# A decoder trunk on one core: the down projection also computed with seven block products for eight

## The chip, the cores and the metric

The kernel runs on one core of a Trainium2 chip. The metric is the device time of one execution in microseconds. TensorE does the matmuls, VectorE (DVE in the rows) and ScalarE (ACT) the element-wise work, GpSimd (POOL) little, and SyncE (SP) issues all loads of weights from HBM. An engine executes its instructions in program order; engines wait for each other by semaphores.

## The reference, cut to what matters

Two layers act on 256 tokens of width 2048. Layer 0 is a state-space mixer, layer 1 an attention over shared keys and values; each is followed by the same feed-forward part, and a norm ends the whole:

```
def swiglu(u, w_gate, w_up, w_down):
    return (jax.nn.silu(u @ w_gate) * (u @ w_up)) @ w_down
...
        u = rmsnorm(h, g_ffn[i])
        h = h + swiglu(u, w_gate[i], w_up[i], w_down[i])
```

D_FF is 5632, so gate and up are 2048 x 5632 matrices and down is 5632 x 2048, all float32. The change concerns the product with `w_down`, in both layers.

## The kernel before, in words

**Jobs.** The matmul work is a list of jobs (`add`), run in order by `run_stream` (lines 146 to 155). A job usually owns one weight tile of 512 input rows by 512 output columns, 1 MB, laid out as 128 partitions x 4 blocks (`kb`) x 512. For float32 accuracy each operand is split in two parts, hi (rounded to fp32r, by a ScalarE copy) and lo (the rest, by a VectorE subtraction), and a product is three matmuls: hi x hi, lo x hi, hi x lo (`mm3`, lines 128 to 137). The activations are the stationary operand (128 x 128), the weights the moving one (512 columns). A tile has 4 blocks and two halves of 128 tokens (`a`), so a job is 4 x 2 x 3 = 24 matmuls.

**Split and load.** `split_upto` (lines 96 to 115) splits a tile in two units of 128 x 1024: hi on ScalarE (line 111), lo on VectorE (line 112). The hi and lo buffers hold four units, so a unit's buffer is free when the matmuls of the unit four before are done. Tiles come through a ring of three `raw` buffers, loaded by SP (line 90), asked for two jobs ahead of their split. The order on every engine is the order of the program: matmuls of job i, then `split_ahead(i)` (lines 118 to 126; the split of job i+1, and of a further job where both together have at most three units), then the callbacks hung on job i (`pend`, `after`).

**Gate and up.** The 5632 hidden columns are 11 chunks of 512, done in two halves of 6 and 5 chunks (`PARTS`); after the chunks of a half come the down jobs that read them. The first chunk is 8 plain jobs. The other ten of each layer have 13 jobs: in the first weight tile of gate and up, seven block products stand in for eight (a 2 x 2 block scheme over token halves, halves of the tile's 4 blocks, and gate/up). These seven products (`s_add`, `mm1`, 6 matmuls each, one unit) are at the indices 0, 1, 2, 4, 6, 7, 8 of the chunk as products 1, 6, 7, 5, 2, 3, 4; they read sums of weights made by VectorE in tiles E, F, W (`s_sum`, line 769; T4 is made just ahead of the split of product 4) and sums of activations made once per layer (`s_combine`). The plain jobs are at 3, 5 and 9 to 12. `s_evac` combines results (line 803). `g_rows` (lines 844 to 853) transposes a chunk's result into the operand `g` of the down jobs: four transposes on TensorE, a ScalarE copy to hi (line 852) and a VectorE sub to lo (line 853), for token half 0 behind the job at index 2 of the next chunk, for half 1 behind that at index 3.

**Down.** Before, `ffn` (lines 877 to 921) has a plain loop: four column tiles c, and for each the 6 or 5 tiles of the half, each job with 24 matmuls into two banks of PSUM. Behind a column `add_hr` (two VectorE ops, line 875) adds the result to h. In layer 0's second half, `u_chunk` then transposes the new columns of h for the k jobs of the attention (`hT_blocks`, lines 169 to 181: TensorE, ScalarE line 179, VectorE line 180). PSUM has eight banks: acc0 to acc3, two x, two tr; consecutive chunks alternate between the acc banks (`own`) and x and tr.

The pool `rows` (9 buffers of 128 x 512) holds results between steps; a buffer is handed out again after as many allocations as the pool has.

Of the kernel before, what the change touches and what calls it, by code (L numbers as in the profile page):

```python
# [30 lines left out]
def trunk_kernel(ctx: ExitStack, tc: tile.TileContext, par, x_tok, x_grp, b_st, g_st, c_st, cst, gvec,  # L31
# [5 lines left out]
    keep = ctx.enter_context(tc.tile_pool(name="keep", bufs=1))  # L37
    big = ctx.enter_context(tc.tile_pool(name="big", bufs=1))
    ring = ctx.enter_context(tc.tile_pool(name="ring", bufs=2))
    rows = ctx.enter_context(tc.tile_pool(name="rows", bufs=9))  # L40
    ps = ctx.enter_context(tc.tile_pool(name="ps", bufs=1, space=bass.MemoryType.PSUM))
    ctx.enter_context(tc.manual_schedule())

# [29 lines left out]
    def add(src, t, mm, after=None):  # L73
        j = Job()
        j.src, j.t, j.mm, j.after, j.pre = src, t, mm, after or [], []
        j.part, j.make = None, None
        jobs.append(j)
        return j

# [5 lines left out]
    def load_upto(n):  # L85
        while st["load"] < min(n, len(jobs)):
            j = jobs[st["load"]]
            if j.part is None:
# [7 lines left out]
    def split_upto(n):  # L96
        while st["split"] < min(n, len(jobs)):
            i = st["split"]
            load_upto(i + 3)
            if len(parts) < 2:  # L100
                parts.append([ring.tile([128, 4, 512], F32R, name=f"{nm}{i}", tag=nm) for nm in ("hi", "lo")])
            j = jobs[i]
            if j.make is not None:
                j.make()
            j.hi, j.lo = [], []
            for p in range(units(j)):
                raw = j.raw[:, 2 * p:2 * p + 2] if j.part is None else j.part()
                u = st["unit"]
                st["unit"] += 1
                hi, lo = [t[:, 2 * (u % 2):2 * (u % 2) + 2] for t in parts[u // 2 % 2]]  # L110
                act.activation(hi, raw, AF.Copy)  # L111
                (pool if i < NPRE else dve).tensor_tensor(lo, raw, hi, op=OP.subtract)  # L112
                for k in range(2):
                    j.hi.append(hi[:, k])
                    j.lo.append(lo[:, k])
            st["split"] += 1
# [22 lines left out]
    def mm1(pr, opnd, j, first, join):  # L139
        for kb in range(2):  # L140
# [3 lines left out]
            pe.matmul(pr, oh, j.lo[kb], start=False, stop=first and kb == 1, skip_group_check=join)  # L144

    def run_stream(i0, i1):
        for i in range(i0, i1):
# [36 lines left out]

    def s_combine(un, g):

        SC["c"] = big.tile([128, 2, 4, 2, 128], F32R, name=f"sc_{un}", tag="DA"[un == "u_f1"])
# [500 lines left out]
    def chunk_end(j, f):  # L688
        pend.append((j, f))
# [39 lines left out]

    CT, NT, T, gr = {}, [], {}, {}  # L730

    def gu_acc(nm, own):
# [123 lines left out]
    def r_diag(r):  # L856
        t = row()
# [19 lines left out]
    def ffn(l, un, wg, wu, wd, r, down_evac):  # L877
        for hf, (ca, cb) in enumerate(PARTS):
            for c in range(ca, cb):
                own = (cb - 1 - c) % 2  # L880
                j0 = len(jobs)
                if c == 0:
                    for nm, w in (("gate", wg), ("up", wu)):
                        for kg in range(4):
                            add(w, 4 * c + kg, gu_job(nm, un, own, kg, kg == 0, kg == 3))
                    pend.append((j0 + 4, gate_evac(c, r)))
                    pend.append((j0 + 7, gu_end))
                    pend.append((j0 + 8, up_evac(c)))
                    src = lambda a, c=c: (lambda: sil[c][a])
                else:  # L890
                    pend.append((j0 - 5, s_load(l, c, wg, wu)))
                    pend.append((j0 - 3, S_T1))
                    pend.append((j0 - 2, S_T2))
                    pend.append((j0 - 2, S_T3))
                    X = lambda nm, w, kg: add(w, 4 * c + kg, gu_job(nm, un, own, kg, kg == 1, kg == 3, (0,) if nm == "gate" else (0, 1)))
                    for i in (1, 6, 7):
                        s_add(i, un, own)
                    X("gate", wg, 1)
                    s_add(5, un, own)
                    X("gate", wg, 2)  # L900
# [12 lines left out]
            for c in range(4):  # L913
                for kg in range(k0, k1):
                    add(wd, 11 * c + kg, mm_job(("down", l, hf, c), kg == k0, kg == k1 - 1, g_opnd(l, hf), 4 * (kg - k0)))
                if hf == 0:
                    chunk_end(len(jobs), lambda c=c: add_hr(("down", l, 0, c), c, r))
                else:
                    chunk_end(len(jobs), down_evac(c))
                    if l == 0:  # L920
                        u_chunk(len(jobs) + 1, c, "u_kv", 0)

    def down0_evac(c):
        def f():
# [427 lines left out]
```

## Time and profile before

| what | value |
|---|---|
| median of 3 runs | 2098.48 us (2096.45 to 2098.67) |
| profiled execution, own time | 2097.13 us |
| its span, first to last instruction | 2095.3 us |
| mean granted TensorE clock | 0.995 |
| busy: TensorE, VectorE, ScalarE | 2061.8, 1387.9, 1000.5 us |

The difference between the profiled execution's time and its span is 1.83 us; the median of the runs lies 1.35 us above the profiled one. In the rows further down a timeline row has the start in microseconds from the span's start, the duration, the engine, the line of the kernel, the operation, out<-in, the shape, and in brackets how long the engine had been idle before and what released it. Matmuls are pipelined: one lasts longer than the distance to the next.

### The profile page before, as it was taken

Reading aid. Unit: us, or ns where it says so; the run is one execution under the profiler, and the core shown is the slowest. Engines: PE = TensorE matmul, PEld = TensorE weight load, DVE = VectorE, ACT = ScalarE, POOL = GpSimd, SP = SyncE. Lnnn points to the kernel's source line nnn. Section 1 sums busy time; section 2 is a strip of 40 time slices with the busy share of each in tenths; the row PEclk is TensorE's granted clock in tenths of the full one; section 3 lists DMA queues with packets and bytes.
Section 4 is the critical chain, followed back from the end, with each engine's and each line's share of the span. In section 5 each row is a group of like instructions: output and inputs, shape, how many; then the busy total and the mean of one; then the engine's idle time right before and its main releaser. Section 6 shows DMA issues by size and latency. Waiting matters only on the chain.

```text
span 2095.3 us, 28782 instructions
## 1 busy us (share of the span) xinstructions
PE 2061.8 (98%) x11592; PEld 1736.3 (83%) x11592; DVE 1387.9 (66%) x1941; ACT 1000.5 (48%) x1253; POOL 149.9 (7%) x105
## 2 busy tenths in 40 slices
PE   7999999999999999999999999999999999999998
PEld 6778778888888888889999998788888888888886
DVE  8984977776456777555555555667777546777654
ACT  6344555544434455444444444555455334555443
POOL 7741400000000000000000000000000000000000
PEclk9999999999999999999999999999999999999999
DMA  3034556554565555555544544464564556554454
GB/s 142 23 122 144 199 200 221 188 194 161 201 227 196 179 182 180 201 183 177 183 161 168 178 163 165 172 221 168 199 227 150 199 186 224 215 189 173 174 200 149
DMA packets 54054, 376.20 MB, mean 180 GB/s; under 512 B 6432, under 2 KB 6944, under 8 KB 9120
## 3 DMA queue, kind: packets, MB, share of 16 engines
q1 hardware_dynamic: 53920, 374.36, 50.9%
q8 instruction: 91, 1.49, 0.3%
q14 instruction: 43, 0.35, 0.0%
HBM read 370.14 MB, written 2.10 MB: 178 GB/s over the span
## 4 chain that ended last, share of the span: by engine, by line
PE 92%; DVE 5%; ACT 1%; issue 1%; DMA 1%; SPq 1%; ACTq 0%; POOLq 0%; POOL 0%; DVEq 0%
PE acc L137 16%; PE acc L135 16%; PE acc L136 16%; PE x L137 3%; PE x L135 3%; PE x L136 3%; PE tr L135 3%; PE tr L137 3%; PE tr L136 3%; PE acc L961 3%; PE acc L960 3%; PE acc L959 3%; PE x L524 1%; PE acc L144 1%; PE acc L142 1%; PE acc L143 1%
## 5 line engine op out<-in xcount | busy, mean ns | idle before, releaser
L112 DVE TENSOR_TENSOR lo<-raw,hi 128x1024 fp32r<-128x1024 f32 x594 | 721.1, 1241 | 341.9 <-ACT hi L111 337.2
L111 ACT ACTIVATE hi<-raw 128x1024 fp32r<-128x1024 f32 x608 | 627.2, 1055 | 346.9 <-PE acc L136 248.6
L135 PE MATMUL acc<-hi,g 128*128 128x512 f32 x704 | 274.9, 390 | 0.0
L137 PE MATMUL acc<-lo,g 128*128 128x512 f32 x704 | 274.0, 389 | 0.0
L136 PE MATMUL acc<-hi,g 128*128 128x512 f32 x704 | 274.0, 389 | 0.0
L135 PE MATMUL acc<-hi,u_f 128*128 128x512 f32 x512 | 200.5, 392 | 0.6 <-ACT hi L111 0.5
L137 PE MATMUL acc<-lo,u_f 128*128 128x512 f32 x512 | 199.6, 390 | 0.5 <-DVE lo L112 0.5
L136 PE MATMUL acc<-hi,u_f 128*128 128x512 f32 x512 | 199.4, 389 | 0.0
L137 PEld LDWEIGHTS acc<-lo,g 128*128 128x128 f32 x704 | 132.2, 188 | 27.6
L136 PEld LDWEIGHTS acc<-hi,g 128*128 128x128 f32 x704 | 132.2, 188 | 27.1
L135 PEld LDWEIGHTS acc<-hi,g 128*128 128x128 f32 x704 | 132.2, 188 | 27.0
L111 ACT ACTIVATE hi<-st 128x1024 fp32r<-128x1024 f32 x60 | 63.4, 1056 | 115.2 <-DVE st L769 115.2
L137 PEld LDWEIGHTS acc<-lo,u_f 128*128 128x128 f32 x512 | 96.1, 188 | 21.3 <-DVE lo L112 1.3
L135 PEld LDWEIGHTS acc<-hi,u_f 128*128 128x128 f32 x512 | 96.1, 188 | 20.8 <-ACT hi L111 0.9
L135 PE MATMUL x<-hi,u_f 128*128 128x512 f32 x288 | 113.0, 392 | 0.0
L136 PEld LDWEIGHTS acc<-hi,u_f 128*128 128x128 f32 x512 | 96.2, 188 | 20.0 <-DVE u_f L180 0.3
L137 PE MATMUL x<-lo,u_f 128*128 128x512 f32 x288 | 112.2, 390 | 0.0
L136 PE MATMUL x<-hi,u_f 128*128 128x512 f32 x288 | 112.1, 389 | 0.0
L135 PE MATMUL tr<-hi,u_f 128*128 128x512 f32 x288 | 112.0, 389 | 0.0
L136 PE MATMUL tr<-hi,u_f 128*128 128x512 f32 x288 | 112.0, 389 | 0.0
L137 PE MATMUL tr<-lo,u_f 128*128 128x512 f32 x288 | 112.0, 389 | 0.0
L112 DVE TENSOR_TENSOR lo<-st,hi 128x1024 fp32r<-128x1024 f32 x60 | 73.4, 1223 | 25.7 <-ACT hi L111 24.1
(294 smaller groups left out, 3792.7 us busy)
## 6 DMA issues: line engine op xcount, KB each, us to landing
raw<-w_down SPq DMA_DIRECT2D x88, 1024.0 KB, 4.8
raw<-w_gate SPq DMA_DIRECT2D x68, 1024.0 KB, 4.9
raw<-w_up SPq DMA_DIRECT2D x68, 1024.0 KB, 4.9
raw<-w_kv SPq DMA_DIRECT2D x32, 1024.0 KB, 4.8
su<-w_up SPq DMA_DIRECT2D x20, 1024.0 KB, 4.8
sg<-w_gate SPq DMA_DIRECT2D x20, 1024.0 KB, 7.0
raw<-w_glu SPq DMA_DIRECT2D x16, 1024.0 KB, 4.8
raw<-w_q SPq DMA_DIRECT2D x16, 1024.0 KB, 4.8
```

The source lines that it names most:

```text
L111: act.activation(hi, raw, AF.Copy)
L112: (pool if i < NPRE else dve).tensor_tensor(lo, raw, hi, op=OP.subtract)
L135: pe.matmul(pr, oh, j.hi[kb], start=first and kb == 0 and not jn, stop=False, skip_group_check=jn)
L136: pe.matmul(pr, ol, j.hi[kb], start=False, stop=False, skip_group_check=jn)
L137: pe.matmul(pr, oh, j.lo[kb], start=False, stop=last and kb == 3 and not jn, skip_group_check=jn)
L142: pe.matmul(pr, oh, j.hi[kb], start=first and kb == 0, stop=False, skip_group_check=join)
L143: pe.matmul(pr, ol, j.hi[kb], start=False, stop=False, skip_group_check=join)
L144: pe.matmul(pr, oh, j.lo[kb], start=False, stop=first and kb == 1, skip_group_check=join)
L524: pe.matmul(yb[64 * g2:64 * g2 + 64, g], H[q][r, ri, gl + g2].rearrange("p k c -> p (k c)"), Z[r, :, ri, 2 * (8 * o + g) + b], start=ri == ...
L959: pe.matmul(p, j.hi[kb][:, s], u[:, 0], start=first and kb == 0 and n % 2 == 0, stop=False)
L960: pe.matmul(p, j.hi[kb][:, s], u[:, 1], start=False, stop=False)
L961: pe.matmul(p, j.lo[kb][:, s], u[:, 0], start=False, stop=last and kb == 3 and n % 2 == 1)
```

## The change

Tiles of down are taken in pairs of column tiles (c = 2cp and 2cp + 1). For each pair, the four weight tiles of the half's first two row tiles form a 2 x 2 block matrix, and seven products replace its eight (token halves x row tiles x column tiles). It does so for seven of the eight pairs; the last pair of layer 1 stays plain.

- `down_pair` makes the jobs. A product (`s_job`) has 12 matmuls (`mm1` with n = 4); an `x_job` is a plain tile. The order is written out: `1 B2 5 A2 3 B3 7 6 A3 2 4 B4 A4 A5 B5` (digits are products, A and B the columns), or up to `A4 B4` in the second half. Three of the four weight tiles are loaded whole into E, F and W (`d_load`, three jobs ahead), the fourth through the ring. `whole` makes weight sums on VectorE (two ops of 128 x 1024 each), just ahead of the splits of products 5, 7, 6 and 4. `e1`, `e6`, `e7` and `fold` combine the results (one ScalarE copy, seven VectorE ops a pair).
- `g_combine` makes the sums of activations, called from `g_rows` in the first two chunks of each half: n = 0 and 1 for the first chunk's token halves, 2 and 3 for the second's. It needs the transposed bank `tr`.
- The pool `rows` has 6 buffers, not 9; there are new tiles Q, X0, X1. The parity of `own` in the second halves turns over, and the pairs alternate between the acc banks and x and tr.
- Both `add_hr` of a pair come at its end (behind its last job and the job after), and both `u_chunk` one and two jobs later.

```
-    rows = ctx.enter_context(tc.tile_pool(name="rows", bufs=9))
+    rows = ctx.enter_context(tc.tile_pool(name="rows", bufs=6))
...
+            if c - PARTS[hf][0] < 2:
+                g_combine(2 * (c - PARTS[hf][0]) + a, tr, dst[:, :, b0:b0 + 4])
...
+    def g_combine(n, tr, g):
...
+        def put(i, src):
+            d = SC["g"][i // 2]
+            act.activation(d[:, 0, i % 2], src, AF.Copy)
+            dve.tensor_tensor(d[:, 1, i % 2], src, d[:, 0, i % 2], op=OP.subtract)
+
+        if n == 0:
+            act.activation(X0, tr, AF.Copy)
+        if n == 1:
+            act.activation(X1, tr, AF.Copy)
+            dve.tensor_tensor(X0, tr, X0, op=OP.subtract)
+            put(2, X0)
+        if n == 3:
+            V = v4(row())
+            dve.tensor_tensor(X1, X1, tr, op=OP.subtract)
+            put(0, X1)
+            dve.tensor_tensor(V, tr, X0, op=OP.subtract)
+            put(1, V)
+            t0 = slice(0, 128)
+            dve.tensor_tensor(X0, g[:, 0, :, t0].bitcast(F32), V, op=OP.subtract)
+            dve.tensor_tensor(X0, X0, g[:, 1, :, t0].bitcast(F32), op=OP.add)
+            put(3, X0)
...
+    def d_load(l, hf, cp, wd):
+        def f():
+            k0 = PARTS[hf][0]
+            for t, c, k in (("E", 0, 0), ("F", 1, 0), ("W", 1, 1)):
+                T[t] = big.tile([128, 4, 512], F32, name=f"d{t}{l}{hf}{cp}", tag=t)
+                nc.sync.dma_start(T[t], wd[11 * (2 * cp + c) + k0 + k].rearrange("p (k n) -> p k n", k=4))
+        return f
...
+    def down_pair(l, hf, cp, wd, own, r):
...
+        pend.append((j0 - 3, d_load(l, hf, cp, wd)))
...
+            j = add(wd, 11 * 2 * cp + ca + 1, f)
+            if i != 2:
+                j.home = {1: E, 5: E, 3: W, 7: F, 6: W, 4: W}[i]
+            j.make = {5: whole(E, E, F), 7: whole(F, F, W), 6: whole(W, E, W)}.get(i)
...
+        order = "1 B2 5 A2 3 B3 7 6 A3 2 4 B4 A4 A5 B5" if hf == 0 else "1 B2 5 A2 3 B3 7 6 A3 2 4 A4 B4"
...
+        def e1():
+            T["P"] = row()
+            act.activation(T["P"], acc[keys[0]][0], AF.Copy)
+
+        def e6():
+            T["u"] = row()
+            tt(T["u"], T[6], T["P"], OP.subtract)
+            tt(T["P"], T[5], T["u"], OP.add)
+
+        def e7():
+            t = row()
+            tt(t, T[7], T["P"], OP.add)
+            dve.scalar_tensor_tensor(T["u"], T[7], -1.0, T["u"], op0=OP.mult, op1=OP.subtract)
+            T["x"] = t
+
+        pend.append((pos["1"], e1))
+        pend.append((pos["6"], e6))
+        pend.append((pos["A3"], e7))
+        pend.append((pos["4"], lambda: (fold(T["P"], 0, 1), fold(T["u"], 1, 0))))
+        pend.append((pos["4"] + 1, lambda: fold(T["x"], 1, 1)))
...
-                own = (cb - 1 - c) % 2
+                own = (c + 1) % 2
...
+                down_pair(l, hf, cp, wd, (cp + hf + 1) % 2, r)
+                n = len(jobs)
+                for i in range(2):
+                    c = 2 * cp + i
+                    if hf == 0:
+                        chunk_end(n - 1 + i, lambda c=c: add_hr(("down", l, 0, c), c, r))
+                    else:
+                        chunk_end(n - 1 + i, down_evac(c))
+                        if l == 0:
+                            u_chunk(n + 1 + i, c, "u_kv", 0)
```

## Rows read from the trace of the kernel before

**Rows 1.** The page's busy times and shares by engine, over the span.
```profile
span 2095.3 us, 28782 instructions
...
PE 2061.8 (98%) x11592; PEld 1736.3 (83%) x11592; DVE 1387.9 (66%) x1941; ACT 1000.5 (48%) x1253; POOL 149.9 (7%) x105
```

**Rows 2.** One stretch: us; PE, PEld, DVE, ACT, POOL busy (x); clock; DMA.
```profile
600.00:800.00 200.00, 200.00 (x895) 165.62 (x894) 143.95 (x139) 96.62 (x102) 0.00 (x0) 1.00 0.58 206
```

**Rows 3.** TensorE's waits, 200 to 1500 us: total, times, longest.
```profile
PE acc L135 <- ACT hi L111: 5.8, 3, 3.7
```

**Rows 4.** Timeline of TensorE, first and last matmul of the first down tile.
```profile
514.05 0.39 PE L135 MATMUL acc<-hi,g 128*128 128x512 f32 x1
...
519.26 0.39 PE L137 MATMUL acc<-lo,g 128*128 128x512 f32 x1
```

**Rows 5.** Timeline of ScalarE and VectorE in the first down tiles.
```profile
516.23 2.35 DVE L112 TENSOR_TENSOR lo<-raw,hi 128x1024 fp32r<-128x1024 f32 x2
...
531.29 1.06 ACT L111 ACTIVATE hi<-raw 128x1024 fp32r<-128x1024 f32 x1 [1.66 <-PE acc L136]
...
532.38 1.23 DVE L112 TENSOR_TENSOR lo<-raw,hi 128x1024 fp32r<-128x1024 f32 x1 [1.27 <-ACT hi L111]
```

**Rows 6.** Timeline of one gate/up chunk, three engines, index 3 to 6.
```profile
391.88 0.68 DVE L853 TENSOR_TENSOR g<-acc,g 128x512 fp32r<-128x512 f32 x1
...
395.99 0.69 DVE L853 TENSOR_TENSOR g<-acc,g 128x512 fp32r<-128x512 f32 x1 [0.56 <-ACT g L852]
...
396.56 0.39 PE L135 MATMUL x<-hi,u_f 128*128 128x512 f32 x1
...
396.94 1.23 DVE L112 TENSOR_TENSOR lo<-sg,hi 128x1024 fp32r<-128x1024 f32 x1 [0.26 <-ACT hi L111]
398.08 0.68 DVE L803 TENSOR_TENSOR row<-tr,row 128x512 f32<-128x512 f32 x1
398.68 1.22 DVE L112 TENSOR_TENSOR lo<-su,hi 128x1024 fp32r<-128x1024 f32 x1
399.82 1.22 DVE L769 TENSOR_TENSOR st<-st,sg 128x1024 f32<-128x1024 f32 x1
...
401.15 1.06 ACT L111 ACTIVATE hi<-st 128x1024 fp32r<-128x1024 f32 x1 [3.29 <-DVE st L769]
...
402.24 1.23 DVE L112 TENSOR_TENSOR lo<-st,hi 128x1024 fp32r<-128x1024 f32 x1 [1.21 <-ACT hi L111]
```

**Rows 7.** One line's instructions: ScalarE copy in s_combine, ns min/median/max.
```profile
L206 ACT ACTIVATE sc_u_f<-V_u_f x4: 629/631/633, 231.2 to 1333.5; 128x512 fp32r<-128x512 f32 x4
```

**Rows 8.** Timeline of u_chunk at the start of the k jobs, three engines.
```profile
985.24 0.47 ACT L179 ACTIVATE u_kv<-tr,gv 128x256 fp32r<-128x256 f32 x1 [2.79 <-PE tr L175]
...
985.59 0.28 PE L960 MATMUL acc<-u_kv,hi 128*128 128x256 f32 x1
...
985.74 0.48 DVE L180 SCALAR_TENSOR_TENSOR u_kv<-tr,gv,u_kv 128x256 fp32r<-128x256 f32 x1 [1.86 <-ACT u_kv L179]
...
986.26 0.84 ACT L179 ACTIVATE u_kv<-tr,gv 128x256 fp32r<-128x256 f32 x2 [0.55 <-DVE u_kv L180]
...
988.20 0.48 DVE L180 SCALAR_TENSOR_TENSOR u_kv<-tr,gv,u_kv 128x256 fp32r<-128x256 f32 x1 [0.55 <-ACT u_kv L179]
```

**Rows 9.** DMA issues by destination: count, size of one, median us to landing.
```profile
raw<-w_down SPq DMA_DIRECT2D x88, 1024.0 KB, 4.8
...
sg<-w_gate SPq DMA_DIRECT2D x20, 1024.0 KB, 7.0
```

**Rows 10.** Timeline of TensorE near 1335 us, and one stretch's clock.
```profile
1335.12 0.50 PE L135 MATMUL acc<-hi,o 128*128 128x512 f32 x1 [1.73 <-ACT hi L111]
...
1336.38 0.79 PE L137 MATMUL acc<-lo,o 128*128 128x512 f32 x1 [0.53 <-DVE lo L112]
...
1339.53 0.48 PE L135 MATMUL acc<-hi,o 128*128 128x512 f32 x1
...
1336.00:1338.00 2.00, 1.62 (x4) 1.34 (x5) 1.85 (x3) 0.48 (x3) 0.00 (x0) 0.58 0.03 8
```

More of the change, by code (lines that the diff above doesn't have):

```diff
@@ L75, in add @@
         j.src, j.t, j.mm, j.after, j.pre = src, t, mm, after or [], []
-        j.part, j.make = None, None
+        j.part, j.make, j.home = None, None, None
         jobs.append(j)
@@ L87, in load_upto @@
             j = jobs[st["load"]]
-            if j.part is None:
+            if j.part is None and j.home is None:
                 j.raw = ring.tile([128, 4, 512], F32, name=f"raw{st['load']}", tag="raw", bufs=3)
@@ L104, in split_upto @@
                 j.make()
+            if j.home is not None:
+                j.raw = j.home()
             j.hi, j.lo = [], []
@@ L137, in mm3, with mm1 @@
                 pe.matmul(pr, oh, j.lo[kb], start=False, stop=last and kb == 3 and not jn, skip_group_check=jn)
-    def mm1(pr, opnd, j, first, join):
-        for kb in range(2):
+    def mm1(pr, opnd, j, first, join, n=2):
+        for kb in range(n):
             oh, ol = opnd(0, kb), opnd(1, kb)
@@ L143, in mm1 @@
             pe.matmul(pr, ol, j.hi[kb], start=False, stop=False, skip_group_check=join)
-            pe.matmul(pr, oh, j.lo[kb], start=False, stop=first and kb == 1, skip_group_check=join)
+            pe.matmul(pr, oh, j.lo[kb], start=False, stop=first and kb == n - 1, skip_group_check=join)
     def run_stream(i0, i1):
@@ L185, in s_combine @@
     def s_combine(un, g):
-        SC["c"] = big.tile([128, 2, 4, 2, 128], F32R, name=f"sc_{un}", tag="DA"[un == "u_f1"])
+        t = big.tile([128, 4096], F32R, name=f"sc_{un}", tag="DA"[un == "u_f1"])
+        q = big.tile([128, 2, 2, 4, 128], F32R, name=f"sq_{un}", tag="Q")
+        SC["c"] = t[:, 0:2048].rearrange("p (s n b t) -> p s n b t", s=2, n=4, b=2)
+        SC["g"] = [q, t[:, 2048:4096].rearrange("p (s n b t) -> p s n b t", s=2, n=2, b=4)]
+        SC["x"] = [big.tile([128, 512], F32, name=f"sx{n}_{un}", tag=f"X{n}") for n in range(2)]
         for b in range(2):
@@ L730, in trunk_kernel, with pair_banks @@
     CT, NT, T, gr = {}, [], {}, {}
+    def pair_banks(keys, own):
+        tags = ("acc0", "acc2", "acc1", "acc3") if own else ("x", "x", "tr", "tr")
+        b = [bank(t) for t in tags]
+        acc[keys[0]], acc[keys[1]] = b[:2], b[2:]
+        if own:
+            new_acc.n = 1
     def gu_acc(nm, own):
@@ L853, in f @@
             dve.tensor_tensor(dst[:, 1, b0:b0 + 4, ts], tr, dst[:, 0, b0:b0 + 4, ts], op=OP.subtract)
-        return f
+            if c - PARTS[hf][0] < 2:
+                g_combine(2 * (c - PARTS[hf][0]) + a, tr, dst[:, :, b0:b0 + 4])
+        return f
+    def g_combine(n, tr, g):
+        v4 = lambda t: t.rearrange("p (b t) -> p b t", b=4)
+        X0, X1 = [v4(t) for t in SC["x"]]
+        def put(i, src):
[18 more added lines that the diff above has]
+            put(3, X0)
@@ new lines, in d_load, with whole, f @@
+    def d_load(l, hf, cp, wd):
[5 more added lines that the diff above has]
+        return f
+    def whole(o, x, y):
+        def f():
+            dst, a, b = o(), x(), y()
+            for p in range(2):
+                s = slice(2 * p, 2 * p + 2)
+                dve.tensor_tensor(dst[:, s], a[:, s], b[:, s], op=OP.add)
+        return f
@@ new lines, in down_pair, with s_job, f, x_job @@
+    def down_pair(l, hf, cp, wd, own, r):
+        ca, cb = PARTS[hf]
+        keys = [("down", l, hf, 2 * cp + i) for i in range(2)]
+        go = g_opnd(l, hf)
+        j0 = len(jobs)
+        E, F, W = [lambda t=t: T[t] for t in "EFW"]
+        pend.append((j0 - 3, d_load(l, hf, cp, wd)))
+        def s_job(i):
+            if i in (1, 2, 4):
+                k0, a = {1: (0, 0), 2: (4, 0), 4: (4, 1)}[i]
+                o = lambda part, kb: go(part, k0 + kb, a)
+            else:
+                n = {5: 0, 6: 1, 7: 2, 3: 3}[i]
+                o = lambda part, kb: SC["g"][n // 2][:, part, n % 2, kb]
+            def f(j):
+                if i in (5, 6, 7):
+                    tags = ("x", "tr", "x") if own else ("acc0", "acc1", "acc2")
+                    T[i] = bank(tags[i - 5])
+                    mm1(T[i], o, j, True, False, 4)
+                else:
+                    c, a = {1: (0, 0), 2: (0, 0), 3: (1, 0), 4: (0, 1)}[i]
+                    if i == 1:
+                        pair_banks(keys, own)
+                    mm1(acc[keys[c]][a], o, j, i == 1, i == 2, 4)
+            j = add(wd, 11 * 2 * cp + ca + 1, f)
+            if i != 2:
+                j.home = {1: E, 5: E, 3: W, 7: F, 6: W, 4: W}[i]
+            j.make = {5: whole(E, E, F), 7: whole(F, F, W), 6: whole(W, E, W)}.get(i)
+            return j
+        def x_job(c, k):
+            def f(j):
+                mm3(acc[keys[c]], go, 4 * k, j, k == 2, k == cb - ca - 1, joins=(0,) if c == 0 else ())
+            return add(wd, 11 * (2 * cp + c) + ca + k, f)
+        pos = {}
+        order = "1 B2 5 A2 3 B3 7 6 A3 2 4 B4 A4 A5 B5" if hf == 0 else "1 B2 5 A2 3 B3 7 6 A3 2 4 A4 B4"
+        for o in order.split():
+            pos[o] = len(jobs)
+            j = x_job("AB".index(o[0]), int(o[1])) if o[0] in "AB" else s_job(int(o))
+            if o == "2":
+                p2 = j
+            if o == "4":
+                j.make = whole(W, W, lambda p2=p2: p2.raw)
+        def tt(o, x, y, op):
+            dve.tensor_tensor(o, x, y, op=op)
+        def hs(a, c):
+            return h[:, a, 512 * (2 * cp + c):512 * (2 * cp + c) + 512]
+        def fold(t, a, c):
+            dve.scalar_tensor_tensor(hs(a, c), t, r[:, a:a + 1], hs(a, c), op0=OP.mult, op1=OP.add)
+        def e1():
[15 more added lines that the diff above has]
+        pend.append((pos["4"] + 1, lambda: fold(T["x"], 1, 1)))
@@ L912, in ffn @@
             k0, k1 = ca, cb
[L913 to L921, printed above, removed]
+            for cp in range(2):
+                if l == 1 and hf == 1 and cp == 1:
+                    for c in (2, 3):
+                        for kg in range(k0, k1):
+                            add(wd, 11 * c + kg, mm_job(("down", l, hf, c), kg == k0, kg == k1 - 1, g_opnd(l, hf), 4 * (kg - k0)))
+                        chunk_end(len(jobs), down_evac(c))
+                    continue
+                down_pair(l, hf, cp, wd, (cp + hf + 1) % 2, r)
[4 more added lines that the diff above has]
+                        chunk_end(n - 1 + i, lambda c=c: add_hr(("down", l, 0, c), c, r))
+                    else:
+                        chunk_end(n - 1 + i, down_evac(c))
+                        if l == 0:
+                            u_chunk(n + 1 + i, c, "u_kv", 0)
     def down0_evac(c):
```

## The prediction

> **What bounds the kernel now.** I read the page's busy shares first: TensorE has work in 2061.8 of 2095.3 us, VectorE in 66% [rows 1]. A busy TensorE could still be waiting inside, so I looked at a stretch of the feed-forward stages: busy for all 200 us, at full clock [rows 2], and the waits of TensorE between 200 and 1500 us hold a single kind above 2 us [rows 3]. So TensorE is the bound, at full rate, and two things follow. Every matmul removed there is time, and every microsecond by which another engine makes TensorE wait is lost, because nothing gives it back later.
>
> The price of a matmul comes from the timeline: in the first down tile the first of 24 starts at 514.05 and the last at 519.26 [rows 4], 5.21 / 23 = 0.2265 us each. A whole tile (X job) is 5.44 us, a new 12-matmul product (S job) 2.72 us.
>
> What VectorE has to spare is read locally. In plain down tiles a unit's hi waits 1.66 us for TensorE to free a slot, and its lo waits for that hi 1.27 us [rows 5]: VectorE idles. In a gate/up chunk it is otherwise. The sub of the second g_rows starts at 395.99, and behind it come, in program order, lo of product 2, an s_evac sum, lo of product 3, the sum T4, ScalarE's hi of it, and lo of product 4 at 402.24, which ends at 403.47 [rows 6]. The plain job at index 5 starts at 396.56 [rows 6]; its 24 matmuls and the 12 of products 2 and 3 come first, so product 4 starts at 396.56 + 36 x 0.2265 = 404.72, and its third matmul, the first to need lo, at 405.17. That lo is only **1.70 us early**. The chunks that the change touches have the same order of work, so I use this one for all. The slack is the number on which the case turns.
>
> **What is removed.** Seven column pairs lose 12 matmuls each (96 become 84): 84 x 0.2265 = **19.0 us**. [...] The trace's own pitch [rows 4] is used.
>
> **g_combine, chunk two of each half (n = 3).** It runs after the job at index 3 of the next chunk, behind the sub at 395.99, and ahead of the split of product 2. Its steps alternate: subtract, ScalarE copy, lo; V, copy, lo; X0 twice, copy, lo. Steps from the rows: a 128x512 VectorE op lasts 0.69 and lets the next in after 0.60, a 128x1024 one after 1.14 [rows 6]; a copy from SBUF on ScalarE lasts 0.63 [rows 7]; handing over costs 0.03 (hi ends 402.21, lo starts 402.24) to 0.11 (T4 ends 401.04, hi starts 401.15) [rows 6]. So: X1 396.60 to 397.29, copy to 397.96, lo 397.99, V 398.59 to 399.28, copy to 399.95, lo 399.98, X0 400.58 to 401.27 and 402.00, copy 402.04 to 402.67, lo 402.70. Only then does ScalarE's queue reach hi of product 2 (402.57 to 403.63, with the 0.1 us overlap of neighbours): lo 403.66, s_evac 404.80, lo of product 3 405.40, T4 406.54 to 407.76, hi 407.87 to 408.93, lo of product 4 at 408.96 in place of 402.24: 6.72 late, less the 1.70: TensorE waits **5.0 us**, in four halves **20.0**. Bounds: with all handovers hidden, seven ops of 0.60 less the 0.33 of idle before 396.94 delay it 3.9 and cost 2.2; the upper end is 5.0 plus the clock (below). I take 5.0, since each queue is in program order and every step needs the one before.
>
> **g_combine, chunk one (n = 0, 1).** Here ScalarE copies the bank that VectorE's g_rows sub has just read. Rows show such a pair kept apart: ScalarE's second block waits 0.55 us for VectorE's sub of the first, in the same bank [rows 8]. So X0's copy starts only after the sub at 391.88 [rows 6]: hi of index 5 moves to 393.1, its second lo to 395.33, the next sub to 396.47, then X1's copy to 397.80, X0 to 398.52, copy to 399.19, hi of product 2 to 400.15, its lo at 400.18, and by the same chain lo of product 4 at 405.48: 3.24 late, less 1.70 is **1.5 us**, in four halves **6.2**. Without that keeping apart the copies would run beside the subs, the delay would be 2.0 and the cost 0.3; 0.3 and 1.5 are the bounds, and I take the upper one because the rows show the wait.
>
> **The pairs.** Per pair VectorE gains eight sums of 1.22, six more lo of 1.23 and seven small ops. Time 0 is the start of product 1. The split of a job is issued one job ahead and needs a slot freed by the job two before. With the order 1 B2 5 A2 3 B3 7 6 A3 2 4 VectorE keeps up to B3, whose second lo starts at 17.38 (slot free at 16.32, plus hi). From there it never rests: sums of 7 (18.52), its lo (20.93, 22.07), sums of 6 (23.21), lo (25.63, 26.77; wanted 27.65), A3 (27.91, 29.05), e6 (30.19), product 2 (31.53, 32.67), e7 (33.81), sums of 4 (35.07, 36.21), hi 36.40 to 37.46, lo 37.49 to 38.71, wanted at 38.08 + 0.45 = 38.53. So 0.2 us late. What follows has room: three folds (0.7 each) run while B4 and A4 take 10.9 us, and add_hr, as many ops as before, moves to the pair's last job and the one after. At the start of a first pair the four s_evac ops and two g_rows subs stand before and between the splits: in the rows lo of the second tile starts at 516.23 behind them [rows 5] and ends at 517.45, wanted, now that the first job is short, at 514.05 + 2.72 + 0.36 of transposes + 0.45 = 517.58; just in time, so nothing. ScalarE's added copy of product 1 (0.6) lies between two hi that are early. Six pairs: 1.2. The seventh, last of layer 0, also carries two u_chunk blocks, each a chain of about 3.4 us between the two engines [rows 8]: by the same walk A2 waits 0.8, product 3 0.3, product 6 0.8, product 4 1.0, so 2.9. Together **4.1**. Lower bound 0; upper 2.5 a pair, if each of its five fed products meets one more half-microsecond handover like that of [rows 8].
>
> **Moved or hidden.** Both u_chunk blocks of the last pair now come one job before the k jobs that read them (after jobs 1 and 2, where one had a column of room and the other a job). In the rows the second k matmul behind the transposes, which will now need lo of the first block, starts at 985.59, and that lo ends at 985.74 + 0.48 = 986.22, handover 0.04 [rows 8]: 0.67 us each, **1.3**, bounds 0 (blocks early) and 3 (the later blocks of the chain wait too). The three loads per pair (E, F, W) cost nothing: as many bytes as before, issued, by the same walk, some 20 us ahead of use, landing in 4.8 to 7.0 us [rows 9]; SP's raw loads behind them find their ring slot free six or more us ahead. If that cover went, a pair would wait for a load, 5 us. The pool of 9 buffers cut to 6: a buffer returns after six allocations, over a chunk, and its last readers are the transposes at index 2 and 3; nothing. Bank parity: nothing, each old bank is read out over a job earlier.
>
> **The sum.** -19.0 + 20.0 + 6.2 + 4.1 + 1.3 = +12.6 us, on the profiled execution's own 2097.13 (span 2095.3): 2109.7. The median of the runs, 2098.48, lies 1.35 above it; I say **2110**.
>
> **Rivals.**
> *The combination hides (faster).* Should ScalarE and VectorE overlap g_combine within the 1.70 us of slack, its 26.2 falls to the lower bounds, 4 x (2.2 + 0.3) = 10.0, or less. It is one place, lo of product 4 in the chunk after; it decides where both blocks together cost 13.6 / 4 = 3.4 us a half, 13.6 being what pairs and k jobs (5.4) leave of the 19.0. Time: 2097.1 - 19.0 + 10.0 + 5.4 = 2093.5; with nothing lost, 2083.5. For: idle VectorE time later in the chunk. Against: both queues are in order and the idle time comes after product 4. Chance 0.14, and 0.11 for an outcome between, about 2100.
>
> *The clock falls in the stalls (slower still).* [...] Chance 0.22.
>
> *The pairs become VectorE's (slower still).* At the upper bound 7 x 2.5 = 17.5 in place of 4.1: 2123. For: VectorE runs some 20 us without a rest, and the start of a first pair has 0.1 us to spare. Against: the walk has it on time to 0.2. Chance 0.13.
>
> The forecast itself, 2104 to 2114, has 0.40. That the change does not remove the work can't be: the matmuls are gone from the code.
>
> **How the numbers follow.** The range 2096 to 2121 leaves out the hidden combination's better half and the worst of the pairs. About 0.2% (4.2 us) is what a measurement of this kernel can tell from no change. Faster by more, under 2094.3: 0.12 of the first rival's 0.14. Within it: 0.02 of that and 0.11 between, 0.13. Slower: 0.40 + 0.22 + 0.13 = 0.75.
>
> **What would show it.** TensorE's matmuls fall by 84. Eight waits of TensorE on lo or hi appear in gate/up chunks, two chunks in each half: about 5 us in the later, 1.5 in the earlier, split over products 2, 3 and 4. In the pairs, small waits at product 4; at the start of the k jobs two of 0.7. The prediction is wrong if lo of product 4 in those chunks comes less than 2 us late, if the pairs show waits over 2 us each, or if TensorE waits for a load.

## The result and the profile after

The changed kernel takes **2117.44 us** (median of 4 runs, 2113.41 to 2122.83); the kernel before, on the same chip, 2097.88. The ratio of after to before is 1.0096, 95% interval 1.0072 to 1.0119: slower by about 1%, as forecast in sign, inside the range of 2096 to 2121, and 7 us above the forecast of 2110.

The profiled execution of after took 2113.41 us (span 2111.3, against 2095.3 before). Its page, the lines that answer to [rows 1], and below them the same stretch of 200 us as [rows 2]:

```profile
span 2111.3 us, 28945 instructions
PE 2058.3 (97%) x11508; PEld 1720.3 (81%) x11508; DVE 1548.0 (73%) x2124; ACT 1054.6 (50%) x1326; POOL 150.9 (7%) x105
```

```profile
600.00:800.00 200.00, 196.29 (x864) 159.95 (x863) 160.23 (x162) 101.01 (x110) 0.00 (x0) 0.99 0.52 187
```

84 matmuls are gone (11592 to 11508), yet the span is 16.0 us longer: TensorE now has gaps, 3.7 us of them in a stretch where it had none.

TensorE's waits between 200 and 1500 us (total, times, longest), where before has one kind above 2 us, that of [rows 3]:

```profile
PE acc L137 <- ACT hi L113: 5.9, 3, 3.7
PE acc L144 <- ACT hi L113: 5.6, 4, 1.5
PE acc L146 <- DVE lo L114: 3.6, 7, 0.5
...
PE tr L1002 <- DVE u_kv L182: 1.8, 1, 1.8
PE x L144 <- ACT hi L113: 1.7, 3, 0.6
...
```

The first line is the wait that was there before. L144 and L146 are the first and third matmul of a product (`mm1`): products wait for hi, then for lo. The line with L1002 (`r_rows`, at the start of the k jobs) is a wait that the prediction does not have.

**Where the time went.** The profiled executions of before and after, part by part, from first to last matmul of each; the four gate/up and the four down parts are those of layer 0's two halves and layer 1's two:

| part | predicted, us | after less before, us |
|---|---|---|
| gate/up, with g_combine | 20.0 + 6.2 = +26.2 | 7.05 + 6.85 + 6.85 + 6.87 = +27.6 |
| down, 84 matmuls less, pairs | -19.0 + 4.1 = -14.9 | -4.68 - 2.66 - 4.61 - 2.03 = -14.0 |
| start of the k jobs | +1.3 | +4.4 |
| up to the first feed-forward matmul | 0 | 249.58 - 250.60 = -1.0 |
| the rest of the attention | 0 | -1.4 |
| end | 0 | +0.4 |
| span | +12.6 | +16.0 |

Of the three parts predicted at 0, -1.4 is the fall of the clock of [rows 10], which the execution of before had and that of after has not (its clock is 1.00 from 1343 to 1353 us, behind the same two waits of 1.72 and 0.53). The -1.0 is within what the start scatters by: in the profiled executions here the first feed-forward matmul comes between 249.3 and 253.8. The +0.4 stands behind the issue of the last output transfer, in every execution with the change (the program ends 8.9 us after the start of the last matmul, against 8.55 in before and in e7_rows6 below); no run shows its cause. In the second row 0.8 of the saving is moved work: eight transposes of `u_chunk` now stand in the gap of the k jobs, and there they make 0.8 of the 4.4.

The single losses agree. A loss is what the starts of two neighbouring matmuls lie apart beyond the pitch of 0.2266, less the 0.19 a chunk that before too loses at its transposes (where a loss is given "in all" further down, the 0.19 is in it): the four chunks with n = 3 lost 5.12, 5.11, 5.09 and 5.15, those with n = 0 and 1 lost 1.62, 1.67, 1.65 and 1.68; five pairs 0.34 or 0.35, the last of layer 1 0.63, the last of layer 0 3.19, together 5.6.

This is the chunk with n = 3, VectorE and ScalarE from the sub of the second `g_rows`, and the matmuls that waited; it answers to [rows 6]:

```profile
353.75 0.69 DVE L867 TENSOR_TENSOR g<-tr,g 128x512 fp32r<-128x512 f32 x1 [0.56 <-ACT g L866]
354.35 0.68 DVE L890 TENSOR_TENSOR sx_u_f<-sx_u_f,tr 128x512 f32<-128x512 f32 x1
355.06 0.63 ACT L879 ACTIVATE sq_u_f<-sx_u_f 128x512 fp32r<-128x512 f32 x1 [1.35 <-DVE sx_u_f L890]
355.73 0.69 DVE L880 TENSOR_TENSOR sq_u_f<-sx_u_f,sq_u_f 128x512 fp32r<-128x512 f32 x1 [0.70 <-ACT sq_u_f L879]
...
360.31 1.04 ACT L113 ACTIVATE hi<-sg 128x1024 fp32r<-128x1024 f32 x1
360.43 0.69 DVE L880 TENSOR_TENSOR sc_u_f<-sx_u_f,sc_u_f 128x512 fp32r<-128x512 f32 x1 [0.69 <-ACT sc_u_f L879]
361.40 0.50 PE L144 MATMUL acc<-hi,u_f 128*128 128x512 f32 x1 [1.49 <-ACT hi L113]
362.66 0.80 PE L146 MATMUL acc<-lo,u_f 128*128 128x512 f32 x1 [0.53 <-DVE lo L114]
...
366.68 1.23 DVE L114 TENSOR_TENSOR lo<-st,hi 128x1024 fp32r<-128x1024 f32 x1 [1.21 <-ACT hi L113]
367.96 0.50 PE L146 MATMUL acc<-lo,u_f 128*128 128x512 f32 x1 [0.53 <-DVE lo L114]
```

From the sub of `g_rows` to lo of product 4 it was 402.24 - 395.99 = 6.25 us; now it is 366.68 - 353.75 = 12.93, 6.68 later. The prediction had 6.72. VectorE and ScalarE take turns: VectorE is idle 0.70 at each copy, ScalarE 1.35 and more at VectorE's steps, with hi of product 2 (360.31) behind the last copy.

The loads of `d_load` are there, and no matmul waits for one; count, size and time to landing, as in [rows 9]:

```profile
dE<-w_down SPq DMA_DIRECT2D x7, 1024.0 KB, 7.0
dF<-w_down SPq DMA_DIRECT2D x7, 1024.0 KB, 9.0
dW<-w_down SPq DMA_DIRECT2D x7, 1024.0 KB, 11.0
```

### The profile page after: what moved, and what is told of

The parts are those of the page before. It is cut to its first block, busy times and chain, and to the rows that moved or that the text cites. A ratio compares the mean times of both kernels' runs of the same rounds, so it can differ in the third digit from the quotient of the medians.

```text
span 2111.3 us, 28945 instructions
## 1 busy us (share of the span) xinstructions
PE 2058.3 (97%) x11508; PEld 1720.3 (81%) x11508; DVE 1548.0 (73%) x2124; ACT 1054.6 (50%) x1326; POOL 150.9 (7%) x105
## 4 chain that ended last, share of the span: by engine, by line
PE 80%; DVE 12%; ACT 4%; issue 3%; DMA 0%; SPq 0%; ACTq 0%; POOL 0%; POOLq 0%; DVEq 0%
PE acc L139 12%; PE acc L138 12%; PE acc L137 12%; DVE lo L114 5%; PE tr L139 4%; PE tr L137 4%; PE tr L138 4%; PE x L138 3%; PE x L137 3%; PE x L139 3%; PE acc L1106 3%; PE acc L1107 3%; PE acc L1105 3%; ACT hi L113 3%; PE acc L146 2%
## 5 line engine op out<-in xcount | busy, mean ns | idle before, releaser
L114 DVE TENSOR_TENSOR lo<-raw,hi 128x1024 fp32r<-128x1024 f32 x552 | 666.9, 1242 | 202.8 <-ACT hi L113 199.3
L113 ACT ACTIVATE hi<-raw 128x1024 fp32r<-128x1024 f32 x566 | 575.9, 1053 | 200.0 <-PE acc L138 107.8
L137 PE MATMUL acc<-hi,u_f 128*128 128x512 f32 x608 | 238.0, 392 | 0.6 <-ACT hi L113 0.5
L139 PE MATMUL acc<-lo,u_f 128*128 128x512 f32 x608 | 237.2, 390 | 0.7 <-DVE lo L114 0.7
L138 PE MATMUL acc<-hi,u_f 128*128 128x512 f32 x608 | 237.0, 390 | 0.0
L139 PE MATMUL acc<-lo,g 128*128 128x512 f32 x256 | 99.9, 390 | 0.5 <-DVE lo L114 0.5
L137 PE MATMUL acc<-hi,g 128*128 128x512 f32 x256 | 100.0, 391 | 0.0
L138 PE MATMUL acc<-hi,g 128*128 128x512 f32 x256 | 99.7, 390 | 0.0
L137 PE MATMUL x<-hi,u_f 128*128 128x512 f32 x240 | 94.4, 393 | 0.0
L138 PE MATMUL x<-hi,u_f 128*128 128x512 f32 x240 | 93.5, 390 | 0.0
L137 PE MATMUL tr<-hi,u_f 128*128 128x512 f32 x240 | 93.5, 389 | 0.0
L138 PE MATMUL tr<-hi,u_f 128*128 128x512 f32 x240 | 93.5, 389 | 0.0
L1105 PE MATMUL acc<-uq,hi 128*128 128x256 f32 x256 | 74.0, 289 | 0.0
L1105 PE MATMUL acc<-u_kv,hi 128*128 128x256 f32 x256 | 73.3, 287 | 0.1
```

The source lines that it names most:

```text
L137: pe.matmul(pr, oh, j.hi[kb], start=first and kb == 0 and not jn, stop=False, skip_group_check=jn)
L1105: pe.matmul(p, j.hi[kb][:, s], u[:, 0], start=first and kb == 0 and n % 2 == 0, stop=False)
```

## The experiments

The theory after the result: the loss is `g_combine` in a stretch where product 4 has 1.70 us to spare, and that work would be free a few jobs later. Rivals: VectorE lacks the time wherever the work stands; the clock, not the waits, makes the difference. Every ratio below is to runs of the kernel before on the same chip as the run.

**The combination later in the chunk (e1_defer).** The subtractions and the copies hang on the job at index 9 of the second chunk (those of n = 0 and 1) and of the third (n = 3), the lo parts on index 10; nothing is left out.

```
-                g_combine(2 * (c - PARTS[hf][0]) + a, tr, dst[:, :, b0:b0 + 4])
+                GB[2 * (c - PARTS[hf][0]) + a] = (tr, dst[:, :, b0:b0 + 4])
...
+                    for n, f in enumerate(g_combine(c - ca)):
+                        pend.append((e + 7 + n, f))
```

> The changed kernel, with g_combine's steps taken out of g_rows and put behind the job at index 9 (subtractions and copies) and index 10 (the lo subtractions) of the same chunk; the same instructions, none left out. Theory A (the place is the cost: the steps stand ahead of product 4, which has 1.7 us to spare): the stalls of 5.1 and 1.65 us in each half go, 27 us, so 2117.4 - 27 = about 2090, faster than the kernel before; the pairs keep 0.3 us each and 3.1 in the last one of layer 0. Rival B (VectorE has too much work, wherever it stands): the work is the same, so the waits turn up at other jobs and the time stays above 2105. Rival C (the clock falls in the stalls carry part of the loss and the spread of the runs): as A, and the spread of the runs falls from 9 us to 2 or 3.

Measured: 2086.39 us (2084.67 to 2087.63), ratio to before 0.9949 (0.9937 to 0.9962); span 2084.6, which is 26.7 less than after's. The same work is now free. TensorE's waits in layer 0's feed-forward part (262 to 960 us), first in after, then in this kernel:

```profile
PE acc L144 <- ACT hi L113: 3.0, 2, 1.5
PE acc L146 <- DVE lo L114: 2.0, 4, 0.5
PE x L144 <- ACT hi L113: 1.1, 2, 0.6
PE x L146 <- DVE lo L114: 1.1, 2, 0.5
PE acc L139 <- DVE lo L114: 1.0, 2, 0.5
PE tr L146 <- DVE lo L114: 0.5, 1, 0.5
```

```profile
PE acc L139 <- DVE lo L114: 1.0, 2, 0.5
PE acc L146 <- DVE lo L114: 0.5, 1, 0.5
PE tr L146 <- DVE lo L114: 0.5, 1, 0.5
```

All waits of products in the gate/up chunks (the L144 lines, most of L146) are gone. The combination, in its new place, and the sub of `g_rows` and lo of product 4 ahead of it:

```profile
352.86 0.69 DVE L867 TENSOR_TENSOR g<-tr,g 128x512 fp32r<-128x512 f32 x1 [0.56 <-ACT g L866]
...
359.11 1.22 DVE L114 TENSOR_TENSOR lo<-st,hi 128x1024 fp32r<-128x1024 f32 x1 [1.21 <-ACT hi L113]
...
365.15 0.68 DVE L900 TENSOR_TENSOR sx_u_f<-sx_u_f,tr 128x512 f32<-128x512 f32 x1
```

Lo of product 4 stands 6.25 behind the sub at 352.86 again, as before the change, and the combination runs 6 us behind it. VectorE has the time; it was the place. So the change is worth about 10 us once this one thing is put elsewhere.

**The same place, other order (e2_reorder).** For n = 3 VectorE does all four subtractions first, ScalarE each copy as soon as its source is there, and the three lo come last: VectorE no longer waits for the copy just made.

```
-            put(0, X1)
+            hi(0, X1)
...
-            put(3, X0)
+            hi(3, X0)
+            lo(0, X1)
+            lo(1, V)
+            lo(3, X0)
```

> The changed kernel, with the steps of n = 3 in another order at the same place: the four subtractions first with each ScalarE copy behind its source, then the three lo, so that no VectorE step waits for the copy just before it. Theory A with its chain of handovers: lo of product 4 comes about 4 us late in place of 6.8, the stall of the later chunk falls from 5.1 to about 2.3 us, in four halves 11 us, so about 2106. If the handovers cost nothing and only the number of operations counts, nothing changes (2117). Rival B: nothing changes.

Measured: 2106.8 us (2103.64 to 2107.41), ratio 1.0045 (1.0033 to 1.0058). Two of the four chunks lost 2.70 and 2.71 in all, the other two 4.30 and 4.32. So about half of the 5.1 was handovers: the 2.5 left are near the lower bound of the prediction (2.2). The 1.6 more in two chunks is the clock: behind the stall of these two it was 0.50 (367 to 369 us and 1490 to 1492, where the matmuls start 0.43 apart), behind that of the other two it stayed at 1.00.

**The copies ahead of the sub (e6_bank).** In chunk one, ScalarE's copy of the bank to X0 or X1 moves ahead of VectorE's sub of the same bank.

```
+            if c == PARTS[hf][0]:
+                act.activation(SC["x"][a].rearrange("p (b t) -> p b t", b=4), tr, AF.Copy)
...
-            act.activation(X0, tr, AF.Copy)
...
-            act.activation(X1, tr, AF.Copy)
```

> The changed kernel, with ScalarE's copies of the transpose bank to X0 and X1 (chunk one of each half) put ahead of VectorE's subtraction from the same bank, in place of behind it. Theory (ScalarE's copy waits for VectorE's read of the same bank, which delays every later hi and lo of that chunk): ScalarE no longer waits 1.2 and 2.4 us for VectorE there, VectorE's subtraction waits 0.6 for the copy in its place, and TensorE's loss in each of the four chunks falls from 1.65 to about 0.9 us; 4 x 0.75 = 3.0 us less, 2114.4. Rival (it is the added work that costs, not the order of the two on the bank): the loss stays between 1.5 and 1.8 us a chunk and the time does not move.

After has these two rows, ScalarE's copies behind VectorE's sub (L867):

```profile
305.55 0.60 ACT L883 ACTIVATE sx_u_f<-acc 128x512 f32<-128x512 f32 x1 [2.38 <-DVE g L867]
310.12 0.60 ACT L885 ACTIVATE sx_u_f<-acc 128x512 f32<-128x512 f32 x1 [1.20 <-DVE g L867]
```

In this kernel the copy stands right behind ScalarE's copy to hi and waits for nothing; the sub starts 0.03 after the copy's end. The second row puts VectorE's wait down to a matmul; in the second half of each layer the profile names the copy itself, with 1.05 us each:

```profile
308.58 0.59 ACT L868 ACTIVATE sx_u_f<-acc 128x512 f32<-128x512 f32 x1
309.20 0.69 DVE L869 TENSOR_TENSOR g<-acc,g 128x512 fp32r<-128x512 f32 x1 [1.06 <-PE tr L145]
```

Each of the four chunks lost 1.10 or 1.11 in all, against 1.80 to 1.86: 0.92 net against 1.65, as expected of the theory. The time is 2114.99 us (2113.23 to 2115.55), ratio 1.0087 (1.0073 to 1.0101), 2.4 below after's median but inside its scatter, and the profiled span is after's 2111.3, since two of its chunks with n = 3 lost 6.9 and not 5.3 (the clock, below); so the rows decide here, not the time. The two reads of the bank follow each other in either order: in after the copy at 305.55 starts 0.04 behind the end of the sub (304.83 + 0.68), here the sub at 309.20 starts 0.03 behind the end of the copy. The order alone moved 0.7 us a chunk.

**The start of the k jobs (e3_kstart, e4_both).** `u_chunk` of layer 0's last pair comes one job earlier; e4_both is this on top of e1_defer.

```
-                            u_chunk(n + 1 + i, c, "u_kv", 0)
+                            u_chunk(n + i + 1 - cp, c, "u_kv", 0)
```

> The changed kernel, with both u_chunk callbacks of the last pair of layer 0 one job earlier (behind the first two k jobs, not the second and third). Theory A: the first 24 jobs' worth after the k jobs' start lose 4.4 us now (two waits of the first k matmuls on a block just made, 0.7 each, and the wait of r_rows for a transpose bank, about 2.2); those of the bank and one of the blocks go, so 2 to 4 us less, 2113 to 2115. Rival: the u_chunk of column 2 only shifts a wait to the job before, no change.

> e1_defer and e3_kstart together. Theory A: both gains add, about 2086 to 2088, 10 us faster than the kernel before. Rival B: above 2100.

Measured: 2119.37 (2116.07 to 2121.09), ratio 1.011 (1.0095 to 1.0126), and 2088.44 (2085.47 to 2091.98), ratio 0.996 (0.9947 to 0.9972). A miss, and the rival of e3_kstart came true: from the first k matmul to the first v matmul it took 25.54 us before, 29.92 after, and 29.32 in both of these. The stall had only moved one gap ahead. The wait in after, then in e3_kstart:

```profile
997.55 1.04 PE L177 MATMUL tr<-cs,h 128*128 128x128 f32 x8
1000.35 0.67 PE L1002 MATMUL tr<-row,ones 128*128 128x256 f32 x2 [1.76 <-DVE u_kv L182]
1001.49 0.66 PE L177 MATMUL tr<-cs,h 128*128 128x128 f32 x4 [0.47 <-ACT R L1003]
```

```profile
984.38 1.03 PE L177 MATMUL tr<-cs,h 128*128 128x128 f32 x8
987.18 0.63 PE L177 MATMUL tr<-cs,h 128*128 128x128 f32 x4 [1.76 <-DVE u_kv L182]
```

The eight transposes of `u_chunk` fill both transpose banks (four go into one). Whatever wants a bank next in the same gap between two k jobs waits 1.76 us until VectorE has read the first out: in after it is `r_rows` and then the transposes of `uq_blocks`, in e3_kstart `uq_blocks` alone. So two users in one gap cost a wait, and moving both blocks by one job leaves two in one gap.

**One user a gap (e5_evac).** On top of e1_defer, layer 0's column 2 is added to h at job n - 2 and transposed at n - 1; column 3 is transposed at n + 1, as before the change.

```
+                        early = l == 0 and c == 2
-                        chunk_end(n - 1 + i, down_evac(c))
+                        chunk_end(n - 2 if early else n - 1 + i, down_evac(c))
...
-                            u_chunk(n + 1 + i, c, "u_kv", 0)
+                            u_chunk(n - 1 if early else n + 1 + (0 if c == 3 else i), c, "u_kv", 0)
```

> The kernel of e1_defer, in which layer 0's third column is added to h two jobs earlier and transposed (u_chunk) one job earlier than there, and the fourth column is transposed where the kernel before did it, so that only one block per gap is left between the last down jobs and the k jobs. Theory (the 4.4 us lost at the start of the k jobs come from two u_chunk columns that hold both transpose banks of PSUM while r_rows and the next transposes want one): the stretch from the first k matmul to the first v matmul falls from 29.9 to 25.5 us as in the kernel before, and the waits of the last pair of layer 0 (3.25 us) stay or shrink by up to 1; time 2086.4 - 4.4 = 2082, ratio 0.993. Rival (the transposes of the fourth column simply wait for the same results of VectorE wherever the third column's block stands): the k stretch stays within 1 us of 29.9 and the time within 2 us of 2086.4, or the wait appears again in the last pair, which then loses over 6 us.

The expectation has two numbers of column 2 the wrong way round: against e1_defer it is added one job earlier and transposed two earlier, as written here. Measured: **2082.73 us** (2082.25 to 2083.11), ratio 0.9934 (0.9922 to 0.9947). The k stretch is 25.62, and `r_rows` and the transposes behind it wait for nothing:

```profile
978.50 1.03 PE L177 MATMUL tr<-cs,h 128*128 128x128 f32 x8
...
985.11 0.59 PE L1022 MATMUL tr<-row,ones 128*128 128x256 f32 x2
985.54 0.60 PE L177 MATMUL tr<-cs,h 128*128 128x128 f32 x4
```

This kernel is faster than after, and by 13.5 us than the one before. Layer 0's last pair still lost 3.23 there.

**The pool alone (e7_rows6).** The kernel before with `rows` of 6 buffers.

```
-    rows = ctx.enter_context(tc.tile_pool(name="rows", bufs=9))
+    rows = ctx.enter_context(tc.tile_pool(name="rows", bufs=6))
```

> The kernel before with the change's smaller pool alone (rows of 6 buffers, not 9). Theory (a buffer comes back over a chunk later, its readers are long done): no new wait of TensorE, 2096.5, within 2 us of the kernel before. Rival (a ring of 6 makes a writer wait for a late reader): a wait of 0.5 us or more in each of the 20 block chunks, 10 us or more slower.

Measured: 2096.93 us against 2096.22 of before, ratio 1.0001 (0.9991 to 1.001). Nothing, as predicted.

**Without the weight sums (e8_nosums).** On top of e1_defer, `whole` makes no sums, so the products read the tiles as loaded and the result is another one.

```
-            for p in range(2):
-                s = slice(2 * p, 2 * p + 2)
-                dve.tensor_tensor(dst[:, s], a[:, s], b[:, s], op=OP.add)
+            return
```

> The kernel of e1_defer without the pairs' weight sums: the products 5, 7, 6 and 4 of a pair read the tiles as they were loaded, so eight of VectorE's 128x1024 sums a pair are left out (and the result is another one). Theory (VectorE works without a rest from B3 to product 4 and is just about 0.3 us late there, 3.25 in the last pair of layer 0): all seven pairs' waits at product 4 go, 6 x 0.34 + up to 3.2, so 2 to 5 us less, 2081 to 2084. Rival (the pairs are VectorE-bound and cost more than the losses that TensorE's gaps show, for instance through the clock): over 8 us less, under 2078. Third possibility (the small waits are ScalarE's or a slot's, not VectorE's sums): within 1 us of 2086.4.

Measured: 2081.29 us (2081.1 to 2082.77), ratio 0.9929 (0.9916 to 0.9943), 5.1 below e1_defer. TensorE's waits between 500 and 960 us, in e1_defer and then here:

```profile
PE acc L146 <- DVE lo L114: 0.5, 1, 0.5
PE tr L146 <- DVE lo L114: 0.5, 1, 0.5
PE acc L139 <- DVE lo L114: 0.5, 1, 0.5
```

```profile
PE acc L139 <- DVE lo L114: 0.5, 1, 0.5
```

Six pairs lost nothing, and the last of layer 0 lost 1.13 in place of 3.25, at A2 and product 3, ahead of the stretch that begins at B3; layer 0's first down part is 5.45 us shorter than before's, just the 24 matmuls (24 x 0.2265 = 5.44). So VectorE's row of work up to product 4 is what the pairs pay for, and they pay about 5 us; the rival of VectorE-bound pairs (17.5) is out.

**The changed kernel again (e9_again, e10_again).** No edit: two more profiled executions, to see why the median lies 4.0 us above the first.

> The changed kernel once more, for a second profiled execution: its median of 2117.44 lies 4.0 us above its profiled execution of 2113.41, in which all four chunks with n = 3 made TensorE lose 5.3 us. Theory (in some executions the granted clock falls in one of those stalls in such a way that the matmuls behind it run slow and the chunk loses 6.9 us in place of 5.3): this execution's span is 2111.3 plus 1.6 for each chunk that lost 6.9, within 0.7 us. Rival (the difference lies elsewhere: the start of the program, a transfer, the pairs): the four chunks lose 5.3 each and the span differs by over 1 us nevertheless.

> The changed kernel for a third profiled execution, with the same expectations: span 2111.3 plus 1.6 for each chunk with n = 3 that lost 6.9 in place of 5.3 us, by the theory of the clock; a difference of over 1 us that these chunks do not show, by the rival.

Measured: 2116.73 us (span 2114.6) and 2113.01 (span 2110.9). In e10_again all four chunks with n = 3 lost 5.3, and the span is within 0.4 of after's. In e9_again one lost 6.88, and that makes 1.6 of the 3.3 us by which it is longer; the expected span, 2112.9, was 1.7 short, more than the 0.7 allowed, so the theory holds for the chunk and not for the whole difference. Of these 1.7, 1.34 is the k stretch (31.26 against 29.92), where the clock fell as well, and the first feed-forward matmul came 0.8 later; small amounts go the other way. The matmuls of product 4 in that chunk and the two-microsecond windows of TensorE in e9_again (us, PE, PEld, DVE, ACT and POOL busy, granted clock, DMA):

```profile
1495.01 0.50 PE L144 MATMUL acc<-hi,u_f 128*128 128x512 f32 x1 [1.11 <-ACT hi L113]
...
1496.27 0.56 PE L146 MATMUL acc<-lo,u_f 128*128 128x512 f32 x1 [0.53 <-DVE lo L114]
1496.63 0.63 PE L144 MATMUL acc<-hi,u_f 128*128 128x512 f32 x1
1497.06 0.63 PE L145 MATMUL acc<-hi,u_f 128*128 128x512 f32 x1
```

```profile
1496.00:1498.00 2.00, 1.74 (x5) 1.37 (x6) 2.00 (x3) 2.00 (x3) 0.00 (x0) 0.64 1.03 422
1498.00:1500.00 2.00, 2.00 (x6) 1.56 (x5) 2.00 (x3) 0.78 (x1) 0.00 (x0) 0.51 0.86 311
1001.00:1003.00 2.00, 1.53 (x7) 1.12 (x8) 0.61 (x2) 0.81 (x2) 0.00 (x0) 0.66 0.33 139
1003.00:1005.00 2.00, 2.00 (x11) 2.00 (x11) 0.77 (x2) 1.26 (x3) 0.00 (x0) 0.50 0.03 8
```

The matmuls behind the stall start 0.43 apart at 0.51 of the clock, in place of 0.23. In the two windows of the k stretch after's clock is 1.00.

## Why the prediction was right, and where it was off

**Right: what bounds the kernel, and what decides.** TensorE was the bound at full rate (busy 98% of the span of before, [rows 1]), so the 84 matmuls were worth their 19.0, and the slack of product 4 in the chunk decided the sign. In the walk through `g_combine` lo of product 4 came 6.72 late and cost 5.0, on the chip 6.68 and 5.1; chunk one was to cost 1.5 and cost 1.65; e1_defer shows the cause by moving the work away, e6_bank that the shared bank is part of it. The rival in which the combination hides fell: it would have needed both blocks together under 3.4 us a half, and they cost 6.8. Loads and the pool cost nothing, as said; the banks that alternate were not tried alone, and no wait in the traces points to them.

**Mis-sized: the start of the k jobs, 1.3 predicted, 4.4 measured** (0.8 of it moved transposes, 3.6 waiting). The step that failed is the one that gave each moved `u_chunk` one late lo of 0.67. For the first gap that was right: from the first transpose to the third k matmul it took 992.03 - 990.12 = 1.91 where before has 985.71 - 984.60 = 1.11, 0.8 more. In the second gap 2.8 more were lost. The prediction counted who waits for the block's results, not who waits for its banks: `r_rows` and `uq_blocks` issue behind it in the same gap and need the two banks that it holds. The upper bound of 3 thought of later blocks of the chain and was still too low. e3_kstart shows that the wait follows the second user of a gap, e5_evac that it goes when each gap has one.

**Mis-sized: the pairs, 4.1 predicted, 5.6 measured.** Product 4 was 0.34 late where the walk had 0.2, twice as much in layer 1's last, and the last pair of layer 0 lost 3.19 where it had 2.9. Its waits stand in the four places that the walk names: 0.9 at A2, 0.2 at product 3, 0.9 at 6 and 1.1 at 4. e8_nosums shows that the waits at products 6 and 4 come from VectorE's stretch without a rest, as argued; the first two stay there without the sums, and only this pair, which alone carries `u_chunk` blocks, has them.

**The clock, right in size and only partly as a case of its own.** The forecast's own range was 2104 to 2114; the median lies 3.4 above it, near the 2116 that four falls of 1.6 us would make (2109.7 + 6.4). The 1.6 is an estimate from the kernel before: from 1336.38 to 1339.53 [rows 10] seven matmuls took 3.15 us, and 7 x 0.2265 is 1.59. The rival in which the clock falls in the stalls came true in some executions: where a fall costs, it costs 1.6 (5.3 to 6.9 in e9_again, in e6_bank and, 2.7 to 4.3, in e2_reorder), as estimated. The one run of e2_reorder with a mean clock of 0.996, against 0.994 or 0.995 in the others, took 2103.64, which is 3.2 below the median: what two falls at 1.6 would make. But a fall need not cost: in after's own profile the clock fell in three of the four stalls (to 0.56 at 364 to 366 us, to 0.50 at 755 to 757 and at 1882 to 1884; 1.00 at 1488 to 1492), and yet all lost 5.3; in that of e6_bank it fell in all four, and two of them lost 5.3.

So the 7.4 us between forecast and median fall in two. The profiled execution lies 3.7 above the 2109.7 of the sum, and that it is so little is luck. The three terms were too small by 1.4, 0.9 and 3.1, together 5.4; 2.0 of that went into the parts predicted at 0, most of it the fall of [rows 10] in before (1.4) and the start's scatter (1.0). The median lies 4.0 above the profiled execution. That the 4.0 are two or three falls that cost fits e9_again, where two falls make 2.9 of its 3.3 us, and e1_defer, which is 29.7 us from after by the medians (each against the kernel before on its own chip) and 26.7 by the profiled spans. But the other runs behind the median have no profile, so for them it is inferred. Their mean granted clocks, 0.994 for the two at 2117 and 0.992 for the one at 2122.83, do not settle it: the profiled execution had 0.993, so these two had no lower clock than it, and by the clock only the places of the falls can differ. For the run at 2122.83, 9.4 us above, four falls at 1.6 and 1.3 at the k jobs would not be enough; its cause stays open. The scatter of the runs does not settle it either (9.4 us in after and 3.0 in e1_defer, but 2.3 in e6_bank, which has the stalls too).

## What to carry to other kernels

Work that is added to a tuned stretch is priced by the slack of the next result that the bound engine wants, not by the idle share of the engine that does it: VectorE was idle a third of the time ([rows 1]: busy 66%), and 27 us were lost (26.7 between the spans of after and e1_defer) for want of a place a few jobs later. Where a step is moved, list what else issues in its new gap and which buffers it holds there, PSUM banks first (a wait of 1.76 us here), not only who reads its result. And where two engines take turns on small operations, put all of one engine's first: that alone took half the stall away (5.3 us to 2.7 in e2_reorder, where the clock did not fall).

## What the runs showed of the hardware that was not expected

A fall of the clock cost nothing in one chunk. In after's chunk with n = 3 the granted clock fell right after the first piece of the stall:

```profile
362.00:364.00 2.00, 1.48 (x4) 1.15 (x4) 2.00 (x3) 0.30 (x1) 0.00 (x0) 0.59 0.00 0
364.00:366.00 2.00, 2.00 (x6) 1.52 (x6) 1.47 (x2) 0.41 (x1) 0.00 (x0) 0.56 0.43 70
```

The slow matmuls ran inside time that TensorE would have spent waiting for hi of product 4 anyway: behind them that wait is 0.2 us, where e9_again, whose clock was still 1.00 there (1494 to 1496 us), has 1.11 (the row at 1495.01 above) and a wait for lo of product 3 of 0.5 ahead of it. So the chunk lost 5.31 in all, no more than the chunk around 1490, whose clock stayed at 1.00 (5.28). In e9_again that chunk's clock fell behind the last piece instead, at 1496, with no wait left to swallow it, and it lost 6.88. The same stall thus costs 5.3 or 6.9 from one execution of a kernel to the next.
